# Two blocks on one Trainium2 core: when the modulation weights of block 2 are read and used

## The chip, the cores and the metric

The program runs on one core of a Trainium2 chip. Its engines are TensorE (matmuls; PE in the profile, PEld for its weight loads), VectorE (DVE), ScalarE (ACT), GpSimd (POOL) and the queue that issues the transfers (SP). The metric is the device time of one execution in microseconds; lower is better. All arithmetic that matters is fp32: a product is made of three matmuls on operands that are split into a high and a low part.

## What is computed

The reference is a block 1 (RMS norm, a projection, an RWKV-7 mixer beside a native sparse attention, output projection, gated feed-forward), whose result x is the input of a block 2 of two layers on x and on a context of 256 tokens. In block 2 every norm is modulated, and the modulations come from a product of two small vectors with a large matrix:

```
x = first_block(x, positions, ...)
for l in range(2):
    mod_x = (silu(c) @ w_ada[l] + b_ada[l]).reshape(bn, 1, 9, 1024)
    mod_c = (silu(c_ctx) @ w_ada[l] + b_ada[l]).reshape(1, 1, 9, 1024)
    h_x = half_ffn(h_x, norm_g[l, 0], mod_x[0], mod_x[1], mod_x[2], ...)
    h_c = half_ffn(h_c, norm_g[l, 0], mod_c[0], mod_c[1], mod_c[2], ...)
    ...
```

w_ada[l] is [1024, 9216] in fp32. The context's first feed-forward (h_c of layer 0) needs neither x nor block 1: only the context and modulations 0 and 1 for its norm, and modulation 2 when its result is added.

## The kernel before

Everything is kept feature-major, 128 features by 256 tokens a tile. A weight piece is 512 KB (128 x 1024 fp32). A Stream (L333) loads pieces into a ring of raw buffers (`load`, L342, the transfer is L349), casts the high part on ScalarE (L356) and subtracts it for the low part (L357). Block 1's projection has the stream `s1` with 2 raw buffers and VectorE for the subtraction. The context's work has the stream `sc` (`st_c`) with 3 raw buffers, 2 of each part, and GpSimd for the subtraction. All transfers of all streams are issued by one queue, SP, in one fixed order; a transfer whose buffer is not yet free holds up all behind it. `gemm` (L360; L364 to L366) uses one piece for 24 matmuls of 256 columns.

The modulations of a layer are `Ada.steps` (L1146), a generator. The matrix is cut in five parts of two modulations each (the fifth has one), and a part in 8 row tiles. One step (in L1150) does one row tile: it loads two pieces through `st_c` (one piece in part five) as they are, with no split, and makes four matmuls of 32 rows by 512 columns (L1163; the profile counts each twice). The eighth step of a part also copies, transposes (L1171) and finishes the modulations on VectorE (L1173 to L1181). Layer 0 has 40 steps.

Where steps stand in the program is set by numbers:

- `EARLY` (L36): the parts that go with block 1's projection, here 0 and 1: 16 steps.
- `E0` (L38): how many of them stand ahead of block 1's norm, here 10 (L543). Block 1's projection then goes token-major (two b of four pieces, L567 to L616), and feature-major over 15 column tiles m (L626); one step follows each load of a column tile (L628), so that the last six of the 16 stand at m = 0 to 5.
- `MC` (L37): before which m the context's norm stands (`ready`, L629), here 10.
- `TICK0`, `TICK` (L35): steps after each hidden tile of the context's feed-forward, in its first group of four hidden tiles and in the five others; both 1. What is left of layer 0's 40 steps comes behind the feed-forward (L1612), three of layer 1's behind block 1's feed-forward (`FILL`).

The program is written in this order: block 1 to the end of its mixers, the context's feed-forward, block 1's output projection and feed-forward (`block1_out`), the context's mixer, and then x. The order in which each engine gets its instructions is made when the kernel is built: a list scheduler takes what its own estimate holds for ready, and what stands first in the program goes first. So the context's work fills block 1's waits. On the chip each engine works its list in order.

In the profile's names `m` is a PSUM tile of block 1 and later of x, `f` one of the context's work, `yh, yl` and `yhc, ylc` the split inputs of block 1 and of the context, `hh, hl` a hidden tile, `mixh, mixl` the mixers' output, `in_w1m` and `in_w1s` the weights of the token-major and the feature-major projection, `in_w1o` of the output projection, `in_w1u` of block 1's feed-forward, `in_up`, `in_dn` of the context's, `in_w2s`, `in_w2m` of its mixer, `in_ada` the modulations', `sa` a sum of squares.

Of the kernel before, what the change touches and what calls it, by code (L numbers as in the profile page):

```python
# [17 lines left out]
PSUM = bass.MemoryType.PSUM  # L18
# [11 lines left out]
# the work of the three mixers: projections, and then what goes beside the units of either attention (a group for each).  # L30
# q, k, v, c, u: projections; V, C, U: what one of their tiles still needs; b: bias; t: a step from outside; s: statistics
# [3 lines left out]
TICK, TICK0 = 1, 1  # L35
EARLY = (0, 1)  # L36
MC = 10  # L37
E0 = 10  # L38
# [99 lines left out]
def stat(w, c0, c1):  # L138
    """[K, M] columns c0:c1 as stationary pieces of 128 columns: [M/128, 128, K/128, 128]."""
    w = np.asarray(w)[:, c0:c1]  # L140
    k, m = w.shape
    return np.ascontiguousarray(w.reshape(k // 128, 128, m // 128, 128).transpose(2, 1, 0, 3))


def movp(w):
    """[1024, 512] as moving pieces of 2 row tiles: [4, 128, 2, 512]."""
    w = np.asarray(w)
    return np.ascontiguousarray(w.reshape(4, 2, 128, w.shape[1]).transpose(0, 2, 1, 3))


def upw(a, b):
    """gate and up columns, interleaved by tile: [22, 2, 128, 8, 128]."""
    return np.ascontiguousarray(np.stack([stat(a, 0, FF), stat(b, 0, FF)], 1))


def per_piece(g):
    """column tiles in a down piece of g row tiles"""
    return 1 if g > 4 else 2 if g > 2 else 4


def dnw(w, groups):
    """[2816, 1024]: for each group of row tiles and few column tiles, [128, g, n * 128], one after another."""
# [9 lines left out]
def adaw(w):  # L172
    """[1024, 9216]: pieces [72, 128, 1024] in the order of their use: two modulations at a time, in four parts"""
# [92 lines left out]
def build(tc, A, O, dbg=(), stop=None):  # L266
# [66 lines left out]
    class Stream:  # L333
# [8 lines left out]
        def load(self, src, a, b, i=0):  # L342
            """a piece as it is; other rings than the usual one take the i-th of many at once"""
# [16 lines left out]
    def gemm(pt, w, m0, m1, xs):  # L360
        """pt += columns m0:m1 of a split stationary piece, over the tiles xs of (hi, lo)"""
# [18 lines left out]
    def squares(pp, ps, src, n, late=0, nb=3, scale=None):  # L380
        """sums [128, n / 128] of the squares of src(k), k = 0..7, token-major; the last, late of them, are summed
        by the tensor engine alone"""
# [22 lines left out]
    def stats(pp, ps, src, n, rs, late=0, nb=3):  # L405
        """rs [128, n / 128] = 1 / rms of src(k), k = 0..7, token-major"""
# [4 lines left out]
    def rms(pp, ps, src, n, out, late=0, rs=None):  # L411
        """out(k, bc): bc [128, n] is 1 / rms of src(k), k = 0..7, along the columns"""
# [12 lines left out]
    def norm_split(pp, ps, src, n, yh, yl, sc, sh=None, late=0, rs=None):  # L425
        """src * rstd * sc(k) + sh(k) in parts yh, yl"""
# [57 lines left out]
    # ================= block 1 =================  # L484
    def block1(ps, early, ready):
# [8 lines left out]
        # rope tables from the positions  # L494
# [48 lines left out]
        for _ in range(E0):  # L543
            next(early, None)
        with ExitStack() as e:
# [10 lines left out]
            def rope_in(dst, nh, cos, sin, rows=128, pp=pp):  # L556
                """dst [rows, nh, 64] in place"""
# [9 lines left out]
            # token-major queries, then keys and values  # L567
            for b in range(2):
                pts = [ps(512), ps(512)]
                for kp in range(4):  # L570
                    wh, wl = st.get(A["w1m"][b, kp], 2, 512)
                    for k2 in range(2):
                        k = kp * 2 + k2
                        for t in range(2):
# [3 lines left out]
                            te.matmul(pts[t], yh[:, k, sl], wl[:, k2], start=False, stop=k == KD - 1)  # L578
                for t in range(2):
# [45 lines left out]
            # feature-major: receptance, keys, values, low-rank inputs  # L625
            for m in range(15):  # L626
                w = st.get(A["w1s"][m], 8, 128)
                next(early, None)  # L628
# [27 lines left out]
            # compressed keys and values  # L656
# [143 lines left out]
        with ExitStack() as e:  # L800
# [16 lines left out]
            # decay: log w = -e^-0.5 sigmoid(w0 + tanh(w_lat) w2); running sums in each chunk  # L817
# [21 lines left out]
            def head_rstd(sq, scale, eps, floor, neg):  # L839
                """sum of sq over the 64 features of a head -> (.)^-0.5, over the features of the head, in PSUM"""  # L840
# [22 lines left out]
            # negated, normalised keys  # L863
# [15 lines left out]
            # the bonus r . k_mod r_k, over v  # L879
# [9 lines left out]
            # A~ = -kk P_{t-1}, R~ = r P: [pair, token tile, which, token]  # L889
# [20 lines left out]
            # token-major A~, B^, K^, V  # L910
# [20 lines left out]
            # Gram blocks, transposed [j, i]  # L931
# [28 lines left out]
            # (I - L)^-1 by substitution: a partition is (parity of the columns, head, chunk)  # L960
# [92 lines left out]
            # group norm over a head, bonus, gate  # L1053
# [31 lines left out]
    def block1_out(ps, st, before_last):  # L1085
        mix = b1mix
        xr = lambda k: res[:, k, 0:T]
# [1 line left out]
        with ExitStack() as e:  # L1089
# [20 lines left out]
            # the scale of the output norm, and of the norm that follows it on its result  # L1110
# [11 lines left out]
    # ================= block 2 =================  # L1122
# [14 lines left out]
    class Ada:  # L1137
        """modulations of a layer, feature-major: M [128, 9, 8, (x, ctx)], and GS = g (1 + scale) of its three norms"""
# [45 lines left out]
    # each table's rope rows, with the norm's gains (and the queries' 1/8) folded in  # L1184
# [22 lines left out]
    def qkn(pp, src, nh, seg, t, tab, hl):  # L1207
        """heads [128, nh, 64]: norm, rope, split into hl [128, nh, 2, 64]"""
# [80 lines left out]
    def in_v(l, st, pp, ps, yh, yl, segs, kvs, tab):  # L1289
        """values and keys; returns what is left to do for the keys, a token tile at a time"""  # L1290
# [27 lines left out]
    def in_qc(l, st, pp, ps, yh, yl, seg, t0, tab, QC):  # L1318
        """queries; returns what is left to do, a token tile at a time"""
# [433 lines left out]
```

## Time and profile before

| | |
|---|---|
| median of 3 runs | 2380.18 us (2373.62 to 2383.07) |
| span of the profiled execution | 2382.3 us |
| PE busy, whole span | 96% |
| first column tile of the feature-major projection on PE | 70.8 us |
| first matmul with the compression's weights | 140.6 us |
| first matmul of block 1's output projection | 527.6 us |
| first matmul of block 1's feed-forward, last one | 570.8 us, 788.9 us |
| first matmul of x's feed-forward | 812.4 us |

The profiled execution has no time of its own beside the span; the span lies 2.1 us over the median and inside the range of the runs. The times in the table are starts of matmuls in the trace, from the span's start. PE counts as busy from a matmul's start to its end, and the ends overlap: in a stretch of back-to-back matmuls it is busy throughout, whether their starts lie 0.12 us apart or 0.28. So the number of matmuls in a stretch tells more of PE's speed than the share of busy time.

### The profile page before, as it was taken

How to read it: one execution, taken by the hardware profiler on the slowest of the kernel's cores; microseconds unless marked ns; L12 is line 12 of the kernel's file. 1: busy time of each engine (PE TensorE's matmuls, PEld its weight loads, DVE VectorE, ACT ScalarE, POOL GpSimd, SP SyncE). 2: the span in 40 equal slices, each digit the busy share in tenths (PEclk: the TensorE clock that was granted, in tenths of full speed). 3: DMA queues.
4: the chain of work that ended last, by engine and by line, in shares of the span. 5: the costliest groups of instructions: out<-in, count | busy, mean ns of one | idle time of the engine just before them, and what ended most of it. 6: DMA issues, size and time to landing. Idle time of an engine off the chain costs nothing.

```text
span 2382.3 us, 38350 instructions
## 1 busy us (share of the span) xinstructions
PE 2283.6 (96%) x15317; PEld 1964.1 (82%) x15317; DVE 1374.2 (58%) x2442; ACT 946.8 (40%) x1602; POOL 361.0 (15%) x278
## 2 busy tenths in 40 slices
PE   7999987999999899998999999999999999999998
PEld 3687766888999689997778777798888889778998
DVE  4555566358656766677565333357534347855665
ACT  4334422236444454454543222245322235554443
POOL 2125444444101200002010000011000003200000
PEclk9999998999999899997999999999999999989999
DMA  8865544356554145553166434465523245303554
GB/s 295 283 213 177 177 129 145 108 176 225 181 179 166 62 141 176 174 175 104 41 221 223 159 131 165 138 236 187 195 92 98 92 134 178 116 21 100 185 186 131
DMA packets 114929, 376.25 MB, mean 158 GB/s; under 512 B 18464, under 2 KB 24480, under 8 KB 114752
## 3 DMA queue, kind: packets, MB, share of 16 engines
q1 hardware_dynamic: 114752, 373.82, 47.3%
q8 instruction: 120, 1.97, 0.3%
q14 instruction: 57, 0.47, 0.1%
HBM read 372.20 MB, written 1.57 MB: 157 GB/s over the span
## 4 chain that ended last, share of the span: by engine, by line
PE 65%; issue 23%; DVE 6%; DMA 4%; POOL 1%; ACT 1%; SPq 0%; POOLq 0%; DVEq 0%; ACTq 0%
PE m L364 10%; PE m L366 10%; PE m L365 10%; PE f L364 5%; PE f L366 5%; PE f L365 5%; PE f L1163 3%; DMA r<-in_ada 2%; PE o L1388 2%; PE m L1362 2%; PE f L1378 1%; PE m L1357 1%; POOL sa L398 1%; DVE l L357 1%; ACT h L356 1%
## 5 line engine op out<-in xcount | busy, mean ns | idle before, releaser
L356 ACT CAST h<-r 128x1024 fp32r<-128x1024 f32 (+1 forms) x547 | 567.1, 1042 | 1065.4 <-PE m L365 434.9
L357 DVE TENSOR_TENSOR l<-r,h 128x1024 fp32r<-128x1024 f32 (+1 forms) x467 | 572.3, 1229 | 352.2 <-ACT h L356 343.0
L364 PE MATMUL m<-yh,h 128*128 128x256 f32 (+1 forms) x1624 | 490.2, 303 | 2.3 <-ACT h L356 1.1
L366 PE MATMUL m<-yh,l 128*128 128x256 f32 (+1 forms) x1624 | 489.8, 302 | 1.0 <-DVE l L357 1.0
L365 PE MATMUL m<-yl,h 128*128 128x256 f32 (+1 forms) x1624 | 489.5, 302 | 0.0
L364 PEld LDWEIGHTS m<-yh,h 128*128 128x128 f32 x1624 | 310.1, 192 | 25.9 <-ACT h L356 8.1
L366 PEld LDWEIGHTS m<-yh,l 128*128 128x128 f32 x1624 | 310.2, 191 | 19.8 <-issue 7.1
L365 PEld LDWEIGHTS m<-yl,h 128*128 128x128 f32 x1624 | 310.4, 191 | 15.6 <-issue 3.7
L357 POOL TENSOR_TENSOR l<-r,h 128x1024 fp32r<-128x1024 f32 x80 | 194.2, 2432 | 337.7 <-ACT h L356 318.6
L398 POOL TENSOR_TENSOR sa<-sa,sq 128x256 f32<-128x256 f32 x81 | 86.1, 1064 | 1038.5 <-issue 743.6
L365 PE MATMUL m<-hl,h 128*128 128x256 f32 (+1 forms) x738 | 220.1, 302 | 0.0
L366 PE MATMUL m<-hh,l 128*128 128x256 f32 (+1 forms) x738 | 219.9, 303 | 0.0
L364 PE MATMUL m<-hh,h 128*128 128x256 f32 (+1 forms) x738 | 215.6, 304 | 0.1
L364 PE MATMUL f<-yh,h 128*128 128x256 f32 (+1 forms) x624 | 199.6, 320 | 1.8 <-ACT yh L434 1.1
L365 PE MATMUL f<-yl,h 128*128 128x256 f32 (+1 forms) x624 | 198.0, 317 | 1.2 <-DVE yl L435 1.2
L366 PE MATMUL f<-yh,l 128*128 128x256 f32 (+1 forms) x624 | 197.8, 317 | 0.0
L364 PE MATMUL f<-hh,h 128*128 128x256 f32 (+1 forms) x446 | 138.7, 316 | 14.4 <-DVE ft L461 6.7
L366 PEld LDWEIGHTS m<-hh,l 128*128 128x128 f32 x738 | 139.1, 189 | 8.5 <-issue 1.6
L365 PEld LDWEIGHTS m<-hl,h 128*128 128x128 f32 x738 | 139.7, 189 | 6.7 <-issue 0.4
L364 PEld LDWEIGHTS m<-hh,h 128*128 128x128 f32 x738 | 136.3, 189 | 10.1 <-issue 2.1
L1538 DVE SCALAR_TENSOR_TENSOR res<-m,mod,res 128x256 f32<-128x256 f32 x176 | 79.3, 479 | 111.3 <-PE m L366 111.1
L366 PE MATMUL f<-hh,l 128*128 128x256 f32 (+1 forms) x446 | 135.6, 311 | 1.5 <-POOL l L357 1.5
(509 smaller groups left out, 4120.2 us busy)
## 6 DMA issues: line engine op xcount, KB each, us to landing
r<-in_up SPq DMA_DIRECT2D x252, 512.0 KB, 3.6
r<-in_ada SPq DMA_DIRECT2D x144, 512.0 KB, 4.4
r<-in_dn SPq DMA_DIRECT2D x98, 512.0 KB, 3.6
r<-in_w1u SPq DMA_DIRECT2D x44, 512.0 KB, 3.5
r<-in_dn SPq DMA_DIRECT2D x32, 448.0 KB, 3.3
r<-in_w2m SPq DMA_DIRECT2D x24, 512.0 KB, 4.0
r<-in_w2o SPq DMA_DIRECT2D x24, 512.0 KB, 3.5
r<-in_w1d SPq DMA_DIRECT2D x22, 512.0 KB, 3.5
```

What stands on the lines that cost most here:

```text
L356: s.copy(h, r)
L357: self.e.tensor_tensor(l, r, f32(h), op=OP.subtract)
L364: te.matmul(pt, w[0][:, k, m0:m1], xs[k][0], start=k == 0, stop=False)
L365: te.matmul(pt, w[0][:, k, m0:m1], xs[k][1], start=False, stop=False)
L366: te.matmul(pt, w[1][:, k, m0:m1], xs[k][0], start=False, stop=k == n - 1)
L398: g.tensor_tensor(acc, acc, sq, op=OP.add)
L1163: te.matmul(pt[j * 32:j * 32 + 32], adac[:, k], w[j], start=k == 0, stop=k == KD - 1)
L1357: te.matmul(o, q, kh[:, kv], start=True, stop=False)
L1362: te.matmul(o, q[0:64], kl[0:64, kv], start=False, stop=True)
L1378: te.transpose(pT[:, b * 128:b * 128 + 128], P[:, b * 128:b * 128 + 128], ident)
L1388: te.matmul(po[j * 64:j * 64 + 64], vals(b // 2, b % 2, kvof(2 * pr + j)), PT[j][:, b], start=b == 0, stop=b == nt - 1)
L1538: v.scalar_tensor_tensor(r, pt[:, i * T:i * T + T], ad[l].M[:, m, d, q:q + 1], r, op0=OP.mult, op1=OP.add)
```

## The change

The diff also blanks comments and docstrings; the rest of it is this:

```
-TICK, TICK0 = 1, 1
-EARLY = (0, 1)
-MC = 10
-E0 = 10
+TICK, TICK0 = 1, 2
+EARLY = (0,)
+MC = 12
+E0 = 2
...
                             te.matmul(pts[t], yh[:, k, sl], wl[:, k2], start=False, stop=k == KD - 1)
+                next(early, None)
                 for t in range(2):
...
             for m in range(15):
                 w = st.get(A["w1s"][m], 8, 128)
-                next(early, None)
+                if m % 3 == 2:
+                    next(early, None)
                 if m == MC:
                     ready()
```

Only part 0 (8 steps, 16 pieces) is now done with block 1's projection: two steps ahead of the norm, one behind each b of the token-major projection, one at m = 2, 5, 8 and 11. The context's norm stands at m = 12. Part 1 goes into the first group of the context's feed-forward, two steps behind each of its four hidden tiles. The five other groups have one step behind a hidden tile as before, 18 in all, so that 6 steps of layer 0, not 2, stand behind the feed-forward. What is computed, and all counts, stay as they are. The lines behind the change move by one or two (L1163 is L1165 in the changed kernel).

How the built lists moved, at three places. The SP queue in block 1's projection, ten transfers from the second column tile's neighbourhood on. Before:

```order
L349 DMA r_219<-in_ada 128x1024
L349 DMA r_625<-in_w1s 128x1024
L349 DMA r_236<-in_ada 128x1024
L349 DMA r_238<-in_ada 128x1024
L349 DMA r_670<-in_w1s 128x1024
L349 DMA r_244<-in_ada 128x1024
L349 DMA r_715<-in_w1s 128x1024
L349 DMA r_246<-in_ada 128x1024
L349 DMA r_586<-in_ada 128x1024
L349 DMA r_588<-in_ada 128x1024
```

and now:

```order
L349 DMA r_558<-in_w1s 128x1024
L349 DMA r_595<-in_w1s 128x1024
L349 DMA r_640<-in_w1s 128x1024
L349 DMA r_960<-in_ada 128x1024
L349 DMA r_2573<-in_up 128x1024
L349 DMA r_2579<-in_up 128x1024
L349 DMA r_677<-in_w1s 128x1024
L349 DMA r_2646<-in_ada 128x1024
L696 DMA wkv_268_1335<-in_wkv 128x256
L349 DMA r_2648<-in_ada 128x1024
```

Column tiles now follow each other; up to this place, that is for the first 30 entries, the two lists are the same. Behind the rows shown the old list has 12 more ada pieces before the last column tile, the new one has one.

PE at the end of block 1's output projection, from its last matmul to the first of the feed-forward (L388 sums squares, L421 spreads the norm's scale; `f` is the context's norm, `m` block 1's). Now:

```order
L366 MATMUL m_5482<-mixh_147,l_5479 128x256
L1165 MATMUL f_7924<-r_7925,sc_82 32x512 x2
L1165 MATMUL f_7924<-r_7927,sc_82 32x512 x2
L1165 MATMUL f_7924<-r_7933,sc_82 32x512 x2
L388 MATMUL f_8023<-ones_67,sa_8024 128x1 x2
L388 MATMUL m_5514<-ones_67,sa_5515 128x1 x2
L1165 MATMUL f_7924<-r_7935,sc_82 32x512 x2
L421 MATMUL f_8054<-sq_8051,ones_67 128x256
L421 MATMUL m_5545<-sq_5542,ones_67 128x256
L1165 MATMUL f_7924<-r_7941,sc_82 32x512 x2
L1165 MATMUL f_7924<-r_7943,sc_82 32x512 x2
L364 MATMUL m_5595<-yh_5508,h_5585 128x256
```

In the old list 79 matmuls of the context's mixer stand there in place of the six ada pieces, of which these surround the scale:

```order
L366 MATMUL f_8172<-yhc_8017,l_8169 128x256
L364 MATMUL f_8172<-yhc_8017,h_8168 128x256
L365 MATMUL f_8172<-ylc_8018,h_8168 128x256
L366 MATMUL f_8172<-yhc_8017,l_8169 128x256
L421 MATMUL m_5545<-sq_5542,ones_67 128x256
L364 MATMUL f_8209<-yhc_8017,h_8205 128x256
L365 MATMUL f_8209<-ylc_8018,h_8205 128x256
L366 MATMUL f_8209<-yhc_8017,l_8206 128x256
```

So the context's norm now meets block 1's norm there, and its mixer comes later.

GpSimd at the end of block 1's feed-forward, between the sum for the output norm's scale (`rsx`) and the second sum (`sa_7981`), on which x's first norm waits. Before:

```order
L398 TENSOR_TENSOR sa_7953<-sa_7953,sq_7973 128x256
L409 TENSOR_TENSOR rsx_5248<-rsx_5248,mhalf_69 128x2
L398 TENSOR_TENSOR sa_7981<-sa_7981,sq_7983 128x256
L398 TENSOR_TENSOR sa_7981<-sa_7981,sq_7986 128x256
L398 TENSOR_TENSOR sa_7981<-sa_7981,sq_7989 128x256
```

and now:

```order
L398 TENSOR_TENSOR sa_7953<-sa_7953,sq_7973 128x256
L357 TENSOR_TENSOR l_8397<-r_8394,h_8396 128x1024
L409 TENSOR_TENSOR rsx_5248<-rsx_5248,mhalf_69 128x2
L357 TENSOR_TENSOR l_8415<-r_8412,h_8414 128x1024
L398 TENSOR_TENSOR sa_7981<-sa_7981,sq_7983 128x256
L357 TENSOR_TENSOR l_8435<-r_8432,h_8434 128x1024
L398 TENSOR_TENSOR sa_7981<-sa_7981,sq_7986 128x256
L357 TENSOR_TENSOR l_8470<-r_8467,h_8469 128x1024
L1217 TENSOR_TENSOR hss_8505<-hss_8505,mhalf_69 128x8
L398 TENSOR_TENSOR sa_7981<-sa_7981,sq_7989 128x256
```

Four splits of the mixer's weights (L357) have come in between. On PE, 36 matmuls of 512 columns (L1261 to L1263) and 48 of 256 of the context's mixer now stand between the last matmul of the feed-forward and x's first one, where there were none of these. Counted in the lists ahead of the first matmul of the output projection, the context's feed-forward has 1584 matmuls before and 1396 now, the modulations 134 of 512 columns and 32 of 256 (part five's) before and 128 and 0 now; ahead of the RWKV part's first matmul (L823) the feed-forward has 722 and 564, the modulations 108 and 80; ahead of the compression's weights 41 and 35, and 64 and 32; ahead of the first column tile the modulations have 40 and 32. (A piece is two of these matmuls of 512 columns, or four of 256; the modulations' weights of part five come last.)

## Rows read from the trace of the kernel before

**Rows 1.** Page, part 1: busy time of each engine, share of span, instructions.

```profile
span 2382.3 us, 38350 instructions
PE 2283.6 (96%) x15317; PEld 1964.1 (82%) x15317; DVE 1374.2 (58%) x2442; ACT 946.8 (40%) x1602; POOL 361.0 (15%) x278
```

**Rows 2.** Windows: length; PE, PEld, DVE, ACT, POOL busy (records); PEclk; DMA share; GB/s.

```profile
0.00:70.80 70.80, 51.89 (x209) 25.51 (x209) 32.80 (x83) 29.45 (x55) 13.49 (x20) 0.95 0.82 293
70.80:140.60 69.80, 69.80 (x514) 57.74 (x513) 43.06 (x79) 29.22 (x48) 7.32 (x22) 1.00 0.78 263
...
168.50:290.10 121.60, 116.58 (x906) 95.92 (x904) 66.18 (x153) 50.55 (x120) 59.90 (x28) 1.00 0.54 178
290.10:527.60 237.50, 214.24 (x1554) 178.33 (x1553) 132.59 (x247) 61.52 (x93) 106.00 (x58) 0.94 0.42 135
...
557.20:570.80 13.60, 12.37 (x88) 11.86 (x87) 9.85 (x16) 8.62 (x17) 10.22 (x7) 0.87 0.66 205
570.80:788.90 218.10, 218.10 (x1734) 214.01 (x1733) 140.97 (x222) 99.51 (x146) 31.31 (x16) 1.00 0.52 172
788.90:812.60 23.70, 14.01 (x47) 9.57 (x46) 15.90 (x42) 11.86 (x29) 10.86 (x13) 0.59 0.12 42
```

**Rows 3.** Waits of SP, 0 to 140 us: total, times, longest.

```profile
SPq L349 <- PE f L1163: 52.3, 27, 5.4
```

**Rows 4.** Windows of line L1163 alone: PE busy (records), PEld busy (records).

```profile
70.80:140.60 69.80, 12.62 (x48) 1.73 (x48) 1.00 0.78 263
140.60:527.60 387.00, 35.86 (x204) 5.73 (x204) 0.96 0.47 154
```

**Rows 5.** PE timeline: start, duration, instruction, [idle before <- releaser].

```profile
51.55 0.39 PE L576 MATMUL m<-h,yh 128*128 128x512 f32 x1
51.87 1.05 PE L1163 MATMUL f<-r,sc 128*32 128x512 f32 x4
52.85 0.50 PE L577 MATMUL m<-h,yl 128*128 128x512 f32 x1
...
66.79 1.05 PE L1163 MATMUL f<-r,sc 128*32 128x512 f32 x4 [0.65 <-DMA r<-in_ada]
...
69.58 1.05 PE L1163 MATMUL f<-r,sc 128*32 128x512 f32 x4 [1.14 <-DMA r<-in_ada]
...
124.73 0.28 PE L364 MATMUL m<-yh,h 128*128 128x256 f32 x1
124.85 0.28 PE L365 MATMUL m<-yl,h 128*128 128x256 f32 x1
...
501.81 0.64 PE L1163 MATMUL f<-r,sc 128*32 128x256 f32 x8
```

**Rows 6.** SP timeline, the last column tiles' loads and the one behind them.

```profile
115.70 10.21 SPq L349 DMA_DIRECT2D r<-in_w1s  x4
128.63 0.33 SPq L349 DMA_DIRECT2D r<-in_wk  x1
```

**Rows 7.** ACT: a wait from 140.6 to 527.6 us, and its timeline.

```profile
ACT h L356 <- DMA r<-in_up: 28.2, 11, 7.9
...
156.25 1.04 ACT L356 CAST h<-r 128x1024 fp32r<-128x1024 f32 x1 [4.18 <-DMA r<-in_up]
...
158.53 0.26 ACT L700 ACTIVATE kc<-m 32x128 f32<-32x128 f32 x1
```

**Rows 8.** POOL timeline at the two joins behind block 1's mixers and feed-forward.

```profile
563.80 2.37 POOL L357 TENSOR_TENSOR l<-r,h 128x1024 fp32r<-128x1024 f32 x1
...
790.15 4.42 POOL L398 TENSOR_TENSOR sa<-sa,sq 128x256 f32<-128x256 f32 x4 [1.28 <-ACT sq L394]
...
796.60 5.76 POOL L398 TENSOR_TENSOR sa<-sa,sq 128x256 f32<-128x256 f32 x7
```

**Rows 9.** DVE timeline: one line at two places.

```profile
13.61 0.48 DVE L419 TENSOR_SCALAR sq<-cst,rs 128x128 f32<-128x128 f32 x2 [0.31 <-POOL rs L409]
...
563.85 2.60 DVE L419 TENSOR_SCALAR sq<-cst,rs 128x128 f32<-128x128 f32 x2 [0.68 <-POOL rs L409]
```

## The prediction, made before the changed kernel ran

> **What bounds the kernel now.** I read the page's busy shares first, then the windows, then the waits and timelines at the places where the change acts. PE is busy for 2283.6 of 2382.3 us [rows 1], so the total can only move by PE's idle time, by work that PE does slowly, and by filler that is where nothing can use it. The windows [rows 2] say where that is. Up to 70.8 us PE has 51.89 us of 70.80 with DMA at 0.82; this is the start. From 70.8 to 140.6 (15 column tiles) it is busy throughout. From 168.5 to 290.1 it has 116.58 of 121.60, and then 214.24 of 237.50: here block 1's mixers are a chain of short steps, and the context's feed-forward is the filler between them. At the first join, 557.2 to 570.8, it has 12.37 of 13.60, nearly all filler. From 570.8 to 788.9 nothing is idle. At the second join, 788.9 to 812.6, it has 14.01 of 23.70 us at a granted clock of 0.59: too little filler is left there. So the filler has a use at the second join, has been worth its time at the first, and in the stretch full of PE work it is only in the way.
>
> **What the change does, part by part.** The work of the whole program stays; each term is what a stretch up to a landmark gains or loses. Counts are those of the lists.
>
> (a) *Up to the first matmul with the compression's weights.* 16 pieces of the modulations leave. Four stood ahead of the first column tile. One piece among matmuls of 512 columns puts the neighbours 1.30 us apart (51.55 to 52.85), where 0.32 (51.55 to 51.87) is the step without it [rows 5]; so a piece costs 0.98 us, four 3.9. Two pieces there also came late, 0.65 and 1.14 us of waiting [rows 5], together 5.7. The other twelve stood among the column tiles: 48 records, 12.62 us [rows 4]. Six of the context's matmuls also leave, at 0.12 us each (124.73 to 124.85) [rows 5]: 0.7. Sum 5.7 + 12.6 + 0.7 = 19.0. What could hide this gain: the tiles' own transfers. At the end, where few ada pieces are left, SP issued four tiles' loads in 128.63 - 115.70 = 12.93 us, 3.2 us for a tile [rows 6]; 15 of them are 48.5 us, and 69.8 - 13.3 = 56.5 leaves room for that and for 8 us of other work. SP waited 52.3 us in 27 waits for a buffer that an ada matmul held [rows 3]; that wait is what goes. Least: the four early pieces were under other waits and the tiles stay a little apart, -13. Most: the tiles come at their work of 24 x 0.12 = 2.9 us, 15 x 0.3 = 5 us more, -24. I take **-19**, the row of the pieces' own time.
>
> (b) *From there to the first matmul of the output projection (387 us).* Up to the RWKV part's first matmul 722 - 564 = 158 fewer matmuls of the context are listed, less the six above: 152 x 0.12 = 18.2 us; the modulations have 48 in place of 44, two pieces more, each 35.86 / 204 x 4 = 0.70 us [rows 4]: 1.4. So 16.8 us less work where PE has 116.58 of 121.60 us [rows 2]. In the part behind it 30 matmuls fewer (3.6 us), eleven pieces more (7.7 us) and part five's eight pieces fewer, at 0.64 [rows 5] 5.1 us: -1.0, and there PE idles by 23 us anyway, so I count it as nothing. The least gain is 0: the filler's own feed can pace the lists, since ScalarE casts the context's weights in the same line as the chain's steps, and waited 28.2 us for their landing in 11 waits; one of 4.18 us stands just ahead of the chain's kc at 158.53 [rows 7]. The most is the work and the idle time of the stretch, 16.8 + 5.0 = 21.8. I take 0.7 of the work, **-12**, since PE is busy for 96% there, nearer to the end at which its work sets the time.
>
> (c) *Work that has moved behind the first matmul of the output projection.* 1584 - 1396 = 188 of the context's matmuls at 0.12, 22.6 us; three pieces at 0.70, 2.1; eight of part five at 0.64, 5.1. All lands where PE has no idle time until the second join: **+30**. This is the same work that (a) and (b) lost; they must get it back.
>
> (d) *First join.* 79 matmuls of the context's mixer (9.5 us) fill it now [rows 2]; six ada pieces, 4.2 us, take their place, so 5.3 us of the join go empty. The context's own norm meets block 1's there, and both sum squares on POOL, seven adds in 5.76 us [rows 8]; if the context's stand ahead, the join grows by up to that. On the other side two splits of 2.37 us [rows 8] no longer delay block 1's scale. Ends 0 and +10; **+5**.
>
> (e) *Second join.* 36 matmuls of 512 columns (twice 0.12, an estimate from the 256-column step) and 48 of 256 are now there: 8.6 + 5.8 = 14.4 us of work in a join that had 9.7 us idle and a slow clock [rows 2]. Against it four splits at 2.37 us stand in POOL's list among the adds of the second sum, which x's scale waits for: 9.5 us, of which POOL's idle 1.28 us [rows 8] takes the first. -14.4 + 8.2 = **-6**. Ends: -14, when the splits fall into the adds' own waits, and +2, when x is held for all four and the matmuls, at that clock, don't fit.
>
> Sum: -19 - 12 + 30 + 5 - 6 = -2, on the profiled 2382.3 us 2380.3. The median of the runs lies 2.1 us below that execution, so the forecast is 2378. The context's norm, put at m = 12, waits for modulations that are ready earlier than before; the adder of the context's first group needs modulation 2, which now comes out of the steps within that group; the lists put them ahead of it, and the adder is off block 1's chain, so both cost nothing as long as the filler is not short.
>
> At (e) and (d) a row bears on GpSimd beside VectorE: the two small operations of L419 took 0.48 us at 13.61, and 2.60 at 563.85 with POOL's split running from 563.80 to 566.17 [rows 8, 9]. [...]
>
> **Rivals.**
> 1. *The chain takes all of it.* PE's work sets the stretch from 140.6 to 527.6, (b) -20, and the mixer's splits at the second join fall into waits, (e) -12: -19 - 20 + 30 + 5 - 12 = -16, 2364. For it: 96% busy. Against it: the 23 us idle behind 290 show a chain with latencies of its own. 0.28.
> 2. *Slower: the filler's feed paces the chain.* ScalarE's casts stand ahead of chain steps and wait for transfers; the chain stretch keeps its 387 us although 17 us of PE work left it. Then the moved work is pure loss: -17 + 0 + 30 + 9 - 2 = +20, 2400. It decides from the point where (b) gives under 8 us of the 17 (then over 12 us slower). For it: the 28.2 us of waits [rows 7]. Against it: with fewer pieces of the context in the stretch, and SP freed sooner, the transfers have more room. 0.17.
> 3. *VectorE stands still under the splits.* At the second join four splits block x's scale and split on VectorE by 2.60 - 0.48 = 2.1 us each, as at 563.85 [rows 9]: +8.5 on the sum, 2386. [...] 0.07.
> 4. *The change doesn't do what it says*: the column tiles stay apart since each waits for its own two raw buffers, (a) -10: 2387. Against it: 3.2 us a tile at the end of the stretch [rows 6]. 0.04.
>
> **How the numbers follow.** Forecast 0.44 (own range 2368 to 2389, from terms that are each off by some 5 us), rivals 0.28, 0.17, 0.07 and 0.04. Within 0.5%, some 12 us and about what a measurement of this kernel can tell from no change, lie the forecast, rivals 3 and 4, less a tail on either side. Faster: rival 1 and 0.04 of the forecast, 0.32. Slower: rival 2 and 0.03, 0.20. Same: 0.48. The range leaves out the lower part of rival 1 and the upper part of rival 2, some 0.1 each: 2359 to 2399.
>
> **What the profile after would show.** (a) right: the first column tile some 5 us earlier, the stretch to the compression's weights near 56 us, SP's wait for ada matmuls well under 52.3 us. (b) right: the output projection's first matmul at 527.6 - 31 = 497; if it stands at 508, rival 2; at 488, rival 1. (c): first to last matmul of block 1's two parts longer by some 30 us, less what the second join takes. (d): 13.6 us become 14 to 20. (e): the second join about 30 us long, busy for over 25, its clock above 0.59. Wrong altogether would be a change of PE's pace in the stretches behind x, which no term here counts, or a transfer of the modulations that holds SP, and with it block 1's weights, at the new first group.

## The result, and the profile after

The changed kernel takes 2408.25 us (median of 4 runs, 2402.7 to 2413.87) against 2379.3 before; the ratio is 1.0116, 95% interval 1.0095 to 1.0136. It is slower by 1.2%, some 28 us, where 2 us less was forecast. The profiled execution spans 2404.7 us, 22.4 more than the one of before. The other 6 us lie in the spread of the runs. PE was busy longer, for the same number of instructions (page, part 1, after):

```profile
span 2404.7 us, 38323 instructions
PE 2291.8 (95%) x15317; PEld 1970.5 (82%) x15317; DVE 1378.5 (57%) x2442; ACT 947.0 (39%) x1602; POOL 357.5 (15%) x278
```

The windows of after, cut at the same landmarks as [rows 2] (length; PE, PEld, DVE, ACT, POOL busy; granted clock; DMA share; GB/s):

```profile
0.00:67.50 67.50, 46.91 (x196) 26.13 (x197) 33.16 (x83) 30.02 (x56) 13.59 (x21) 0.95 0.81 296
67.50:127.10 59.60, 58.00 (x452) 57.04 (x450) 44.99 (x76) 27.60 (x46) 6.88 (x22) 0.94 0.52 183
...
149.50:270.10 120.60, 110.03 (x806) 88.03 (x804) 61.34 (x146) 46.12 (x113) 50.33 (x23) 0.93 0.49 173
270.10:506.00 235.90, 218.81 (x1506) 173.84 (x1505) 127.20 (x240) 60.03 (x88) 100.62 (x53) 0.96 0.42 142
506.00:561.20 55.20, 52.58 (x445) 46.94 (x446) 35.52 (x60) 23.34 (x36) 31.50 (x21) 1.00 0.72 249
561.20:572.60 11.40, 9.03 (x40) 3.13 (x38) 5.49 (x15) 3.50 (x8) 3.13 (x4) 0.71 0.74 276
572.60:796.10 223.50, 218.07 (x1747) 214.76 (x1744) 143.56 (x227) 103.82 (x158) 30.64 (x20) 0.99 0.54 182
796.10:825.40 29.30, 20.60 (x107) 16.97 (x105) 15.61 (x34) 13.06 (x24) 22.85 (x19) 0.88 0.10 37
825.40:1055.80 230.40, 227.92 (x1767) 213.17 (x1768) 156.33 (x291) 110.99 (x206) 5.14 (x7) 1.00 0.44 150
```

The output projection is reached 21.6 us earlier (506.0, 527.6 before), and then 55.2 us are spent where it took 29.6. x starts 13.0 us later, and 9 us more go behind that.

The work of PE is the same in both. So I gave every matmul the step that back-to-back rows show (0.12 us for 256 columns; other widths by their columns, which is an estimate: 512 columns stood 0.23 us apart, 796.26 to 796.49 after), summed that as the work of a stretch, and call the rest of its length lost: idle time, slow starts (0.23 us from the first matmul behind a wait to the next, 582.13 to 582.36 after), a lower clock. The sum of the lost time over the whole trace is 322 us before and 345 after, which is the 22 us. By stretch, in us:

| stretch | before: length, work, lost | after | lost, change |
|---|---|---|---|
| to the first column tile | 70.8, 42.1, 28.7 | 67.5, 38.5, 29.0 | +0.3 |
| column tiles | 69.8, 64.6, 5.2 | 59.5, 52.6, 6.9 | +1.7 |
| compression | 27.9, 25.9, 2.0 | 22.4, 20.7, 1.7 | -0.3 |
| sparse attention | 121.6, 102.3, 19.3 | 120.6, 91.3, 29.2 | **+9.9** |
| RWKV | 237.5, 158.9, 78.6 | 235.9, 158.0, 77.9 | -0.7 |
| output projection | 29.5, 27.6, 1.9 | 55.2, 52.3, 2.9 | +1.0 |
| first join | 13.7, 9.8, 3.9 | 11.4, 6.3, 5.1 | +1.2 |
| block 1's feed-forward | 218.0, 214.4, 3.7 | 223.6, 211.8, 11.8 | **+8.1** |
| second join | 23.6, 3.5, 20.1 | 29.3, 15.2, 14.1 | **-6.0** |
| x's first feed-forward | 223.6, 203.0, 20.6 | 230.4, 205.2, 25.2 | **+4.6** |
| behind it | 1346.3, 1208.0, 138.3 | 1348.8, 1208.0, 140.9 | +2.6 |

**Beside the sparse attention** 11 us of work left and 1.0 us of time. Its first 40.5 us show why; before and after:

```profile
168.50:209.00 40.50, 38.82 (x296) 32.22 (x295) 22.39 (x58) 15.34 (x39) 21.38 (x10) 1.00 0.58 183
```

```profile
149.50:190.00 40.50, 35.52 (x221) 26.02 (x220) 17.00 (x49) 11.92 (x35) 9.35 (x4) 0.79 0.45 163
```

GpSimd's operations there are the splits of the context's weights: ten before, four after. PE had 193 of the context's matmuls before and 96 after, and its granted clock was 0.79, where it had been 1.00. Twice in these 40.5 us it was 0.50 for a while, the first time behind two modulation pieces and matmuls of 16 columns, the second behind two waits for VectorE (0.74 and 0.89 us):

```profile
152.90:163.10 10.20, 7.76 (x37) 7.48 (x37) 4.51 (x13) 1.52 (x3) 4.48 (x2) 0.50 0.58 207
173.40:180.20 6.80, 6.19 (x25) 3.30 (x24) 3.28 (x5) 2.89 (x7) 4.66 (x2) 0.50 0.44 151
```

By the same step, the matmuls in these 17.0 us are 4.7 us of work. At the granted clock of 0.50 matmuls of 256 columns stand 0.21 us apart (159.61 to 159.82), for 0.12, and a piece of the modulations takes 1.9 us (177.59 to 179.45), for 1.0 (164.00 to 164.98). Neither takes more than twice as long, so the clock is at most 4.7 of the 9.9 us, and the rest is idle time. SP's timeline says what came instead of weights. After:

```profile
130.89 4.20 SPq L349 DMA_DIRECT2D r<-in_up  x2
135.20 10.62 SPq L349 DMA_DIRECT2D r<-in_ada  x4
146.89 5.82 SPq L349 DMA_DIRECT2D r<-in_up  x2
152.80 12.61 SPq L349 DMA_DIRECT2D r<-in_ada  x4
169.38 0.80 SPq L349 DMA_DIRECT2D r<-in_up  x2
170.27 9.61 SPq L349 DMA_DIRECT2D r<-in_ada  x4
187.43 1.28 SPq L349 DMA_DIRECT2D r<-in_dn  x3
```

and before:

```profile
152.62 0.80 SPq L349 DMA_DIRECT2D r<-in_up  x2
153.53 6.55 SPq L349 DMA_DIRECT2D r<-in_ada  x2
161.20 1.57 SPq L349 DMA_DIRECT2D r<-in_up  x2
168.26 1.55 SPq L349 DMA_DIRECT2D r<-in_ada  x2
172.01 10.18 SPq L349 DMA_DIRECT2D r<-in_dn  x4
```

Four modulation pieces go through a ring of three raw buffers, so SP can issue the fourth only when PE has used the first: its rows of four last 9.6 to 12.6 us, and the next weights come behind them. A piece of weights gives PE 2.9 us of filler (24 matmuls at 0.12), a piece of the modulations 0.9 (before, 14.76 us in 64 records beside the sparse attention, four to a piece). SP waits for a buffer most of the time in both kernels, for GpSimd's splits or the modulations' matmuls (112.9 of 149.4 us from the compression on before, 95.9 of 143.0 after), so it is what passes that has changed, not how long SP waits.

**In the column tiles** the change did what it says. No modulation record is left among them, and SP's wait for these matmuls fell from [rows 3] to

```profile
SPq L349 <- PE f L1165: 22.5, 11, 3.9
```

The tiles' first matmuls stand 2.9 us apart (75.1, 78.0, 80.9, ... 98.1, 101.0). But SP now stands in the tiles' loads, eleven in a row, so the weights behind them are issued 4.0 us after the last tile's start, where that was 1.7 us, and 17.0 us pass between the last tile's start and the compression, where 13.7 did:

```profile
77.53 33.44 SPq L349 DMA_DIRECT2D r<-in_w1s  x11
114.08 0.33 SPq L349 DMA_DIRECT2D r<-in_wk  x1
```

**In block 1's feed-forward** nearly all of the loss lies in the first 14 us. PE makes 60 matmuls there and 99 before; after, and before:

```profile
572.60:586.60 14.00, 9.06 (x60) 8.49 (x57) 13.26 (x26) 5.96 (x13) 5.08 (x6) 0.87 0.47 160
```

```profile
570.80:584.80 14.00, 14.00 (x99) 13.04 (x98) 11.43 (x23) 9.41 (x17) 3.46 (x2) 1.00 0.41 121
```

PE waits for the low part of block 1's own normed input (`yl`), and its clock, 0.87 in these rows, is 0.50 from 583.2 to 586.2, behind that wait. VectorE's timeline there, and GpSimd's:

```profile
572.30 1.27 DVE L435 SCALAR_TENSOR_TENSOR ylc<-y,mod,yhc 128x256 fp32r<-128x256 f32 x3
...
576.85 4.89 DVE L435 SCALAR_TENSOR_TENSOR ylc<-y,mod,yhc 128x256 fp32r<-128x256 f32 x3
581.67 0.41 DVE L432 TENSOR_TENSOR yl<-y,yh 128x256 fp32r<-128x256 f32 x1
```

```profile
576.20 4.87 POOL L357 TENSOR_TENSOR l<-r,h 128x1024 fp32r<-128x1024 f32 x2 [10.23 <-ACT h L356]
```

```profile
582.13 0.39 PE L365 MATMUL m<-yl,h 128*128 128x256 f32 x1 [4.23 <-DVE yl L432]
```

The two norms' operations alternate on VectorE. Three of the context's take 1.27 us, and 4.89 while GpSimd's two splits run; block 1's `yl` stands behind them. It is what [rows 8, 9] showed at 563.85.

**At the second join** four splits stand in GpSimd's chain to x's scale, as in the list, against [rows 8]:

```profile
798.07 1.40 POOL L398 TENSOR_TENSOR sa<-sa,sq 128x256 f32<-128x256 f32 x1 [0.27 <-ACT sq L394]
799.43 2.36 POOL L357 TENSOR_TENSOR l<-r,h 128x1024 fp32r<-128x1024 f32 x1
801.76 0.70 POOL L409 TENSOR_TENSOR rsx<-rsx,mhalf 128x2 f32<-128x2 f32 x1
802.44 2.41 POOL L357 TENSOR_TENSOR l<-r,h 128x1024 fp32r<-128x1024 f32 x1
...
812.43 3.71 POOL L398 TENSOR_TENSOR sa<-sa,sq 128x256 f32<-128x256 f32 x4
```

### The profile page after: what moved, and what is told of

Its sections match the earlier page's. It is cut to its first block, busy times and chain, and to the rows that moved or that the text cites. A ratio compares the mean times of both kernels' runs of the same rounds, so it can differ in the third digit from the quotient of the medians.

```text
span 2404.7 us, 38323 instructions
## 1 busy us (share of the span) xinstructions
PE 2291.8 (95%) x15317; PEld 1970.5 (82%) x15317; DVE 1378.5 (57%) x2442; ACT 947.0 (39%) x1602; POOL 357.5 (15%) x278
## 4 chain that ended last, share of the span: by engine, by line
PE 56%; issue 23%; DVE 6%; POOL 2%; DMA 2%; ACT 1%; POOLq 0%; SPq 0%; DVEq 0%; ACTq 0%
PE m L364 9%; PE m L365 9%; PE m L366 9%; PE f L364 4%; PE f L366 4%; PE f L365 4%; PE f L1165 2%; PE o L1390 2%; PE m L1364 1%; PE f L1380 1%; PE m L1359 1%; POOL sa L398 1%; DVE l L357 1%; DMA r<-in_up 1%; PE m L948 1%
## 5 line engine op out<-in xcount | busy, mean ns | idle before, releaser
L357 DVE TENSOR_TENSOR l<-r,h 128x1024 fp32r<-128x1024 f32 (+1 forms) x467 | 574.0, 1232 | 354.1 <-ACT h L356 345.2
L365 PEld LDWEIGHTS m<-yl,h 128*128 128x128 f32 x1624 | 311.9, 192 | 20.7 <-DVE yl L432 5.4
L366 PEld LDWEIGHTS m<-yh,l 128*128 128x128 f32 x1624 | 311.7, 192 | 13.7 <-DVE l L357 1.3
L357 POOL TENSOR_TENSOR l<-r,h 128x1024 fp32r<-128x1024 f32 x80 | 194.6, 2438 | 388.1 <-ACT h L356 334.6
L364 PE MATMUL f<-yhc,h 128*128 128x256 f32 x400 | 120.9, 303 | 22.5 <-DVE ft L461 11.2
```

The source lines that it names most:

```text
L357: self.e.tensor_tensor(l, r, f32(h), op=OP.subtract)
L364: te.matmul(pt, w[0][:, k, m0:m1], xs[k][0], start=k == 0, stop=False)
L365: te.matmul(pt, w[0][:, k, m0:m1], xs[k][1], start=False, stop=False)
L366: te.matmul(pt, w[1][:, k, m0:m1], xs[k][0], start=False, stop=k == n - 1)
```

## Experiments

Ratios are to the kernel before, with 95% intervals. The kernel before ran along each time (medians 2379.3 to 2382.8 us), the changed kernel only at first, so differences to the latter are good to some 3 us. Line numbers are those of the changed kernel.

### Which part of the change costs: e1_thin_only, e2_move_only

```
e1 (from after)  EARLY = (0, 1); TICK0 = 1; one step at every column tile
e2 (from before) EARLY = (0,);   TICK0 = 2
```

> The changed kernel with both parts again with block 1's projection (16 steps: two ahead of the norm, one behind each b, one at each of the column tiles 0 to 11), one step behind each hidden tile of the context's first group, norm at m = 12. It keeps the new spacing and undoes the move. If the move of part 1 into the context's first group makes the loss, as the stage sums say, this is like the kernel before: 2380 within 8 us. If the new spacing (or the later norm of the context) costs on its own, it lies at 2390 or above.

> The kernel before with part 1 moved into the context's first group (two steps behind each hidden tile), part 0 with its eight steps ahead of the norm, the context's norm at m = 10 as before. If the move makes the loss: 2400 to 2412, as the changed kernel. If the spacing or the norm's place at m = 12 makes it: 2380 to 2390.

e1: 2391.1 us, 1.0056 (1.0033 to 1.0079). e2: 2407.0 us, 1.0112 (1.0084 to 1.0141). The move alone makes the whole loss. But the new spacing without it isn't free either, 11 us; it lost nothing beside the sparse attention (16.3 us against 19.3) and 9 us more than before in block 1's feed-forward (12.9 against 3.7).

### What part 1 costs at its place: e3_short_after, e4_short_before

```
             for k in range(KD):
+                if l == 0 and i == 1 and 0 < k < KD - 1:
+                    yield
+                    continue
```

> The changed kernel with part 1 of layer 0 cut to two of its eight row tiles: 12 pieces, 6.3 MB, some 11 us of PE work are left out, nothing else. Theory 1 (feed): each of these pieces takes a place in the context's ring of three raw buffers and on SP as a weight piece does, but gives PE 0.9 us and not 2.9, so the filler thins in the first 40 us beside the sparse attention; without them the context's weights come earlier, and the kernel gains clearly more than the 11 us of work, 17 to 28. Theory 2 (chain): the stretch beside the sparse attention has its own latencies, PE was idle there anyway; the gain is at most the 11 us, the time 2397 or more.

> The kernel before with the same 12 pieces of part 1 left out, where they stand among the column tiles. Both theories: PE is busy throughout there, so it gains the pieces' own 11 us on PE, less what then comes too early, 6 to 12 us. If it gains as much as the changed kernel does by the same cut, the place of part 1 isn't what costs, and theory 1 falls.

e3: 2380.3 us, 28 less than the changed kernel. e4: 2370.0 us, 0.9948 (0.9929 to 0.9967), 10 less than the kernel before. The same 12 pieces cost 28 us in the context's first group and 10 us, their own work, among the column tiles. Fifteen (by the ratios) to 18 of the 28 us (by the medians) are thus the place. In e3 the stretch's first 40.5 us have nine splits and a granted clock of 1.00 again:

```profile
148.00:188.50 40.50, 37.73 (x297) 32.34 (x297) 21.78 (x59) 17.20 (x41) 20.33 (x9) 1.00 0.46 161
```

### The ring: e10_ring4_after, e11_ring4_before

```
-    st_c = Stream("sc", 3, 2, side=R, stack=rs, eng=g, parts=rs2)
+    st_c = Stream("sc", 4, 2, side=R, stack=rs, eng=g, parts=rs2)
```

and single scratch buffers in the context's first norm.

> The changed kernel with four raw buffers, not three, in the context's stream (the context's first norm takes single scratch buffers to make room). From the compression to the RWKV part every kernel so far put 2.85 to 3.2 us to a piece of this stream, weights and modulations counted alike. If the number of raw buffers sets that pace, it falls to about 2.7 us, more of the context's matmuls stand beside the sparse attention and the kernel gains 8 to 15 us: 2391 to 2399. If the pace comes from what works on the pieces (splits, casts, the order of the list), nothing changes: 2402 to 2412.

> The kernel before with the same fourth raw buffer. The stretch beside the sparse attention lost only 19 us there, so by the buffers' theory it gains less than the changed kernel does, 2 to 6 us: 2374 to 2378; by the other nothing.

e10: 2389.6 us, 1.0036 (1.0022 to 1.0050), 18 to 19 less than the changed kernel. e11: 2382.8 us, 1.0005 (0.9988 to 1.0022): nothing. Beside the sparse attention 46 pieces passed in 127.5 us, 2.8 us for one, where the changed kernel had 39 in 120.6, 3.1. The same 40.5 us, in e10:

```profile
142.30:182.80 40.50, 38.93 (x275) 30.80 (x277) 21.23 (x59) 14.16 (x38) 15.55 (x7) 0.96 0.60 216
```

Seven splits, clock 0.96; the stretch lost 17.2 us, not 29.2. So the fourth buffer lets the mixed stream flow faster. In e11 the pace rose as well, 44 pieces in 125.2 us, 2.8 for one, without a gain: the kernel before is not short of filler there. By the sums of the lost time e10 loses 19 us less than the changed kernel: 10 less up to the sparse attention, 12 beside it, 13 in block 1's feed-forward and behind x's start together, against 16 more in the parts between. With the feed restored these two late losses go, and the second join's gain goes with them (8 us); that the output projection loses 8 us more stays open.

### The collision: e5_split_dve, e9_split_dve_before

```
         mixc = mix_tiles()
+        st_c.e = v
         mixer(0, "c", st_c, ...)
```

> The changed kernel with the splits of the context's mixer weights (L357 of the stream sc, 24 of them, behind the context's feed-forward) on VectorE in place of GpSimd. Theory: behind the first join three operations of the context's norm on VectorE took 4.89 us where the same three took 1.27 before them, while GpSimd's split ran, and PE waited 4.23 us for block 1's yl behind them; at the second join four splits of 2.4 us stand in GpSimd's chain to x's scale. Without the splits on GpSimd the feed-forward's stretch shortens by 4 us and the second join by 6 to 9 us: 2394 to 2400. Rival: VectorE, which now has 24 more operations of 1.23 us in those stretches, is what holds them, and the time stays at 2405 or more.

> The kernel before with the same splits on VectorE. If the collision of GpSimd and VectorE at the first join costs there too (L419 took 2.60 us, 0.48 elsewhere), it gains 2 to 4 us; at the second join there are no splits before. 2375 to 2381; a loss would show that VectorE has no room for them.

e5: 2398.1 us, 1.0062 (1.0036 to 1.0088), 10 less than the changed kernel. The feed-forward lost 8.4 us, not 11.8, the second join 10.7, not 14.1. In its first 14 us the feed-forward has 101 matmuls again:

```profile
578.20:592.20 14.00, 12.44 (x101) 11.81 (x98) 12.09 (x29) 6.32 (x14) 0.21 (x4) 1.00 0.48 164
```

VectorE's group of three, in e5:

```profile
578.16 1.27 DVE L435 SCALAR_TENSOR_TENSOR ylc<-y,mod,yhc 128x256 fp32r<-128x256 f32 x3
```

PE's waits for `yl` fell from 4.9 to 1.0 us. So the collision is shown by taking GpSimd's splits away; the order of the two norms stayed. Of the 5 us that it frees, 1.7 are lost again right behind, where PE waits for the splits on VectorE. e9: 2382.4 us, 0.9998 (0.9980 to 1.0015). The collision that is in the kernel before costs nothing that can be measured; my 2 to 4 us were a miss. What a collision cost here depended on the operation that it held: 4.23 us of PE's time behind `yl`, nothing measurable behind L419.

### Fewer or later steps: e6_mid, e7_group1, e12_late_steps_before, e13_late_steps_after

```
e6  steps0 = ad[0].steps(range(5), st_c, psf); 12 of them early, the rest in the feed-forward
e7  fill(TICK if gi > 1 else TICK0)
e12 (from before) fill((0, 0, 1, 2, 2, 2)[gi])
e13 (from after)  fill((2, 0, 1, 2, 2, 2)[gi])
```

> The changed kernel with 12 of the 16 steps with block 1's projection (two ahead, two behind the b's, four at m = 2, 5, 8, 11, four at the drain behind the column tiles), so that four steps of part 1, not eight, go into the context's first group, and two steps stand behind the feed-forward. Feed theory: the loss beside the sparse attention goes by about half, with each piece that leaves the group: 2390 to 2397. If the mere presence of part 1 in the group (its modulation 2 is waited for by the group's adder) made the loss, it stays at 2405.

> The changed kernel with two steps a hidden tile in the context's second group too, so that two steps, not six, stand behind its feed-forward. Feed theory: the pieces again displace weights of the context from the ring, in the stretch beside the sparse attention, and nothing is gained: 2404 to 2415. If the six steps behind the feed-forward make the two norms meet and cost the 8 us in block 1's feed-forward, it gains that: 2396 to 2401.

> The kernel before with the 24 steps that stand in the context's feed-forward put later: none in its first two groups, one behind a hidden tile of the third, two in the others. By the feed theory the context's weights get all places of the ring beside the sparse attention, where each gives PE 2.9 us and a modulation piece 0.9, so the stretch loses less than 19 us and the context is ahead at its end; the pieces meet the RWKV part, where PE idles more. Gain 0 to 10 us: 2370 to 2380. If the pieces cost the same wherever they stand, it is the kernel before; if the RWKV part's chain is held by them, 2385 to 2400.

> The changed kernel with the same: part 1 in the first group as it must be, none in the second, one in the third, two in the others, none behind the feed-forward. By the feed theory it takes 8 pieces from the stretch beside the sparse attention and gives back part of the 10 us lost there, and without steps behind the feed-forward the norms' meeting may move: 2390 to 2400. Otherwise 2405.

| | us, ratio (interval) | lost beside the sparse attention | pieces there: weights, modulations |
|---|---|---|---|
| before | 2379.3 | 19.3 | 25, 16 |
| after | 2408.3 | 29.2 | 21, 18 |
| e6 | 2433.8, 1.0215 (1.0169 to 1.0260) | 36.4 | 19, 21 |
| e7 | 2410.7, 1.0111 (1.0072 to 1.0150) | 39.0 | 16, 23 |
| e12 | 2411.3, 1.0107 (1.0073 to 1.0140) | 20.8 | 25, 7 |
| e13 | 2396.2, 1.0069 (1.0045 to 1.0093) | 25.3 | 22, 12 |

e6 was a miss: its four extra early steps came out behind the column tiles, so more modulation pieces stood ahead of the weights, not fewer; that fits the 36.4 us, but not the 18 us that its RWKV part lost besides, which stay open. e7 gained nothing, as the feed theory has it; but its trace shows both effects, 10 us more lost beside the sparse attention and 5 us less in block 1's feed-forward, so the six steps' place had its price too. In the table the loss falls as the weights' pieces rise, from 39.0 us with 16 to 19.3 with 25. e12 was a miss and bounds the theory: with 7 pieces in place of 16 no more weights came through than before, 25, one in 4.7 us. So the ring's places seem to bind only from about the mix of before on; below it something else, not shown, paces the weights, and the delayed pieces (32 us more work between the output projection's start and x's) are loss. Its runs spread widely, nine of the ten from 2386 to 2421, and its trace is of one at 2398. e13 took 12 us off the changed kernel.

### Do the remedies add up: f1_ring4_dve, f2_ring4_late, f3_ring4_thin, f5_ring4_late_dve, f6_ring4_even

f1 is e10 and e5 together, f2 e10 and e13, f3 e10's ring in e1, f5 all three; f6 is f2 with the steps (2, 1, 1, 1, 2, 2).

> The changed kernel with four raw buffers in the context's stream and the splits of the context's mixer on VectorE, both at once. The buffers gave back some 17 us, the splits some 9. If the two are separate causes, together 24 to 27 us: 2380 to 2385, the whole loss. If the fourth buffer already ends the meeting of the norms, so that the splits have nothing left to free, it stays at 2388 to 2391.

> The changed kernel with four raw buffers and the later steps (none in the second group, one in the third, two in the others, none behind). The later steps gave back 11 us with three buffers. If both act on the same cause, the ring's places beside the sparse attention, together hardly more than the buffers alone: 2385 to 2391. If they add up: 2376 to 2382, as the kernel before or better.

> Both parts with block 1's projection at the new spacing (2391 with three buffers), now with four raw buffers. If its 11 us came from the context's late feed, as in the changed kernel, the buffer gives 8 to 12 us back: 2379 to 2384. If they came from the spacing itself, it stays at 2388 or above.

> The changed kernel with all three remedies: four raw buffers, the later steps, the mixer's splits on VectorE. With buffers and later steps alone (2375) the feed-forward behind the norms' meeting still lost 9.0 us of PE and the one on x 28.7, against 3.7 and 20.6 in the kernel before. If that is the collision of GpSimd with VectorE, the splits give 5 to 10 us more: 2365 to 2370, faster than the kernel before beyond doubt. If it is not, 2373 to 2378.

> Four raw buffers and the steps of the second and third group one each again, two in the last two groups, none behind the feed-forward (the splits on GpSimd). If the gain of the later steps comes from having none behind the feed-forward, it is like the version with none in the second group, 2373 to 2378. If it comes from the places that the second group leaves to the context's weights beside the sparse attention, 2382 to 2389, as with the buffers alone.

f1: 2382.2 us, 1.0023 (0.9995 to 1.0051): the ring and the splits together give back the whole loss but for what can't be told from nothing. Its interval overlaps that of e10, so what the splits add to the ring is not shown. f2: 2375.1 us, 0.9975 (0.9959 to 0.9992); its RWKV part lost 13 us less than before, its part behind x's start 10 more. f6: 2377.9 us, 0.9988 (0.9973 to 1.0003), so most of what the later steps give doesn't depend on the second group. f5: 2375.0 us, 0.9974 (0.9961 to 0.9988): here the splits on VectorE gave nothing, a miss; the feed-forward's loss fell from 9.0 to 6.4 us, and the RWKV part lost 4.6 more, without a cause that I could name. f3: 2388.5 us, 1.0041 (1.0023 to 1.0059), hardly under e1. What e1's spacing costs is therefore not the ring, and stays open.

f2 and f5 are the fastest versions, by 0.25%; that is less than what was called a difference ahead, and their intervals just exclude none.

## Why the prediction was wrong, step by step

The forecast's sum, -2 on the profiled execution, missed the measured +22.4 by 24.4 us: 5.5 in (a), 3.9 in (b), 5.3 in (d), 9.4 in what it did not count, and 0.3 in (c). The step that failed is in (b), the 0.7 of the work that was taken for time because PE is busy for 96%: beside the sparse attention 1.0 of 11.0 us came. Its own miss is small, but it set the filler's feed aside as an end of the range, and the experiments put most of the loss there (15 to 18 us by e3 and e4, 19 by e10).

**(a)** -19 was forecast, -13.5 came (140.6 to 127.1). The pieces' price held: the work of the two stretches fell by 15.6 us, where 17.2 of the 19.0 were work. The tiles came at their own 2.9 us. Not seen was the far side: SP bound in the tiles' loads issues the compression's weights late, and the two waits for modulation pieces ahead of the tiles didn't go (one of 2.75 us stands there now; the first tile came 3.2 us earlier, not 5.7).

**(b)** -12 was forecast, -8.1 came (387.0 to 378.9), and this is the step that failed. 5.5 of the 8.1 us are in the compression. Beside the sparse attention 11 us of work went and 1.0 us of time: "nearer to the end at which its work sets the time" was wrong. Busy for 96% was read as full of work; but PE was busy too with matmuls that stood further apart than by their columns (0.11 us for 16 columns, 168.52 to 168.63 before), or at a lower clock (0.21 us for 256, as above): of the 116.58 us of [rows 2] 102.3 are work at the back-to-back step, and after the change 91.3 of 110.03. The busy time shows PE fuller than it is, by 14.3 us before and 18.7 after. What the stretch lacked after the change was filler, for the ring of three buffers. Rival 2 had the right word, feed, and its point of decision (8 us) lies where the stretch came out. That its +20 lies near the +22.4 is luck in part: it had 0 in (b) and nothing behind x. Its evidence was wrong: ScalarE's waits for `in_up` fell (18.7 us beside compression and attention before, 6.3 after). The places in the ring were the cause, as e3 against e4 and e10 show. A reading was wrong besides: the 204 records of [rows 4] are 140 of 512 columns and 64 of 256, so the 0.70 us of a piece mixes two kinds; a piece of 512 columns is 0.9, and the eleven pieces "behind it" and the six of (d) are 1 to 2 us more than was counted.

**(c)** +30 was forecast; the work from the output projection's start to x's rose by 30.3 us (255.3 to 285.6). Right.

**(d)** +5 was forecast for the join. The join became shorter, 13.7 to 11.4, and the loss came right behind it: the lost time of output projection, join and feed-forward together rose by 10.3 us, just over the upper end of 10. The norms did meet. The price is VectorE's, held by GpSimd's splits, and not GpSimd's adds: 4.9 us of waits for `yl`, with a granted clock of 0.87 in these 14 us against 1.00 in e5. The same three operations took 4.89 us while the two splits ran, 1.27 ahead of them, and 1.27 again in e5, where GpSimd is busy for 0.21 of the 14 us. I weighed this for the second join only (rival 3) and not for the first, where its row was from.

**(e)** -6 was forecast, and the second join's lost time fell by 6.0 us, with its clock 0.88 for 0.59. Right in size, though both terms were smaller: 11.7 us more work, not 14.4, in a join 5.7 us longer, not 8.2. PE is busy for 20.60 us of it, where over 25 was the sign. Rival 3's 8.5 us on top of it didn't come.

**Not counted**: what comes behind x's start, where 9.4 us more were spent, 2.2 of them work that moved there. I had named a change of pace behind x as what would be wrong altogether, and gave it no chance. The context's mixer, now later, runs beside x's feed-forward: VectorE is busy for 156.33 us there, against 149.75 in

```profile
812.40:1036.10 223.70, 223.29 (x1746) 210.17 (x1745) 149.75 (x271) 106.45 (x194) 7.37 (x7) 1.00 0.48 154
```

The loss in x's feed-forward goes with the context's lateness: by the same sums it is 24 to 29 us in the eleven traces that have about as much work there as here, or more, and 18 to 23 in the eight others. VectorE is busy for 155 to 164 us there in the eleven, and for 145 to 152 in the eight. What makes it is argued, not shown. The 2.6 us behind that stretch can't be told from the spread: there, with the same work in all nineteen traces, the lost time varies by 9 us.

In sum: -13.5 - 8.1 + 30.3 of work + 4.3 lost up to x + 9.4 behind it = +22.4. The work went where forecast, and the stretches that it left did not shorten by as much.

## What to carry to other kernels

Filler that shares a ring of buffers is counted in pieces, not in bytes or in PE's time: ask how much work each piece gives the engine that waits (here 2.9 or 0.9 us), and how many pieces pass in a stretch (here 39 in 120.6 us). Before counting a stretch's work as removable, sum its matmuls at their back-to-back step and compare with its length; a busy share near 1 says little (here 0.96 was busy and 0.84 was work). Where late work makes two chains meet on an engine, look at what a third one does to it at that moment.

## What was not expected of the hardware

Three VectorE operations took 4.89 us beside two GpSimd operations of 2.4 us, 1.27 without, so one collision on a chain's critical place cost PE 4.2 us. And a shortage of filler went with two losses, idle time and clock: where only four pieces of weights came in 40 us, the granted clock was 0.79 in the changed kernel (0.87 in e6, also with four); it was 0.96 with seven pieces (e10) and 1.00 with nine (e3).
